# p7 of the first triple among the a products, two multiplications set aside, mixed loads and an earlier hold, in a matmul-tanh-multiply kernel

## The chip, the cores and the metric

The kernel runs on one core of a Trainium2 chip. The metric is the device time of one execution in microseconds (us); the time of a kernel is the median of its runs.

## The reference

```python
# x: (16, 512, 1024), w1, w2: (1024, 768), all float32
y1 = np.matmul(x, w1)
y2 = np.matmul(x, w2)
return (np.tanh(y1) * y2).astype(np.float32)
```

## The kernel before

**Tiles.** The 16 * 512 = 8192 rows of x are 64 row tiles of 128 rows. The 1024 terms of the inner dimension are 8 chunks of 128 (`k`), in two halves of four. The columns of the two weights make three blocks of 512: `a` (the first 512 columns of w1), `b` (the first 512 of w2) and `g` (the last 256 of w1 and of w2 side by side). Operands are fp16, sums are fp32 in eight PSUM banks.

**Two ways to multiply.** The first four row tiles (`HEAD`) are multiplied plainly, chunk by chunk, in chains `a`, `g`, `b` (`mm`, L421; the b chain of row tile 3 is kept for the very end). The other 60 make 20 triples. Three row tiles by two halves of the inner dimension by three column blocks would be 18 products of half an inner dimension each; a bilinear scheme does it in 15 (`p0` to `p14`, four matmuls each, `product`, L444). Its operands are sums of x blocks (`A_SUMS`, made by VectorE per triple, `x_sum`, L412) and sums of weight blocks (`B_SUMS`, made once, `w_sum`, L403). A number names a block or a sum: for x, bits 0 to 5 are the two halves of the triple's three row tiles; for weights, bits 0, 1, 2 are a, b, g of the first half and bits 3, 4, 5 of the second. So p7 (16 by 1) takes the first half of the triple's third row tile and block a; p10 (32 by 8) that tile's second half and block a; p6 (15 by 5) needs all of the first two row tiles, and no b; p1 (3 by 24) needs the second half of b.

**After the products.** A product goes to a bank (`c0` to `c10`). `C_OPS` lists what is made of it: copies from a bank to the SBUF buffer `arena` (`copy376` takes p7's result, ScalarE, L448), additions (`add312` adds that copy to p6's result, in front of p9; VectorE, L454), tanh (ScalarE, L457) and the multiplications `m0`, `m1`, `m2`, `mh0`... by the other half (VectorE, L462). Plain chains have their own: tanh L424, multiplication L428; for row tiles 0 to 2 the b result is copied to a buffer `y` (L431) and multiplied much later (`later_mul`, L435).

**Loads.** SP's queue loads the first four row tiles in halves as float32 (`x00` is row tile 0, first half) and the a and g weights into slots of `arena`; ScalarE's queue loads a0 to a3. VectorE and ScalarE cast them (L359, L357; `cx..`, `ca..`, `cg..`). POOL's queue loads the b weights and all other row tiles, cast to fp16 on the way (L350, L353), first the eight b, then row tiles 6, 4, 5 (`rows_in`), then 7, 8, 9 and on. In front of the first b load POOL waits for the cast of g0 (`gate`, L484), and from row tile 10 on it waits in front of each load (`hold_loads`, L481, a copy of one column) for the transposed tile four before, here T7.

**Transposes.** x must be turned. Row tiles 0 to 6 are turned by TensorE (L371) and copied from PSUM (`evacuate`, L357); from 7 on by DMA from SP's queue (`T7`, ..., L378), in order of row tiles.

**Order.** Nothing here is a loop in the program. A planner in Python (`Planner`) gets every operation with its engines, cost, due time, `needs` and `behind`, simulates the engines, and the instructions are written out in the order it finds. The order of the products on PE is given as a list (`plan.strict`): `FIRST_ORDER` for the first triple from `START`, `PE_ORDER` for the others, where "+" means one triple later. Plain matmuls and transposes are fitted in by the planner. `hold` is the earliest time of an operation in the plan, `lands` when a load is assumed to land. On the chip each engine runs its instructions in the written order and waits on semaphores.

Beside this ScalarE makes sums of absolute values of all inputs (`D..`, `aw..`, L381), which a flag at the end checks.

Of the kernel before, what the change touches and what calls it, by code (L numbers as in the profile page):

```python
# [69 lines left out]
FIRST_ORDER = "7 10 1 6 12 9 11 14 8"  # L70
# [156 lines left out]
def kernel(  # L227
# [14 lines left out]
    F = 512  # L242
# [10 lines left out]
    LANDING = {HEAD + 6: 5.8, HEAD + 7: 4.1, HEAD + 8: 3.9}  # L253
    S_AHEAD, HALVED = 4.0, 4
    LATER = {mt: 66.0 + 13.0 * mt for mt in range(HEAD - 1)}
# [25 lines left out]
    S_NAMES = [o[3] for o in C_OPS if o[1] in ("copy", "add") and o[3][0] == "s"]  # L281
    arena = once.tile([P, len(S_NAMES) * C_BUFS * F], f32, name="arena")
# [3 lines left out]
    early_x = once.tile([P, len(A_SUMS) * S_BUFS * KH * P // 2], f32, name="early_x")  # L286
    x_first = [early_x[:, mt * K:(mt + 1) * K] for mt in range(HEAD)]
# [8 lines left out]
    def xh_place(mt):  # L296
        return (mt - HEAD) % XH_BUFS

    def xh_before(mt):
        return next((m for m in range(mt - 1, 1, -1) if xh_place(m) == xh_place(mt)), None)  # L300
# [35 lines left out]

    def load_first(e, mt, h):
        pin(nc.sync.dma_start(x_first[mt][:, half(h)], xf[mt][:, half(h)]))

    def cast_x(e, mt, h):  # L340
        copy(e, xh(mt)[:, half(h)], x_first[mt][:, half(h)])
# [10 lines left out]
    def load_x(e, mt):  # L352
        pin(nc.gpsimd.dma_start(xh(mt), xf[mt]))  # L353
# [87 lines left out]

    def product(e, i, dst, a, b, begins):
        for k in range(KH):
            pin(nc.tensor.matmul(place(i, dst), x_operand(i, a)[:, k, :], w_rhs(b, k),  # L444
                                 start=begins and k == 0, stop=k == KH - 1, skip_group_check=True))
# [17 lines left out]

    def flag_1(e):
        pin(nc.vector.tensor_scalar(good, sums, HIGH, None, ALU.is_le))
# [14 lines left out]
    def hold_loads(e, mt):  # L480
        pin(nc.gpsimd.tensor_copy(held, xt(mt)[:, 0, :1]))  # L481

    def gate(e, s, k):
        pin(nc.gpsimd.tensor_copy(held, w_cols(s, k)[:, :1]))  # L484
# [5 lines left out]
    START = 28.6  # L490
    ORIGIN = START - 6 * SLOT

# [17 lines left out]
    GATE = ("g", 0)  # L510
    in_order = on_sp[4:] + late + [f"x{mt}" for mt in rows_in]
# [3 lines left out]
    for n in in_order:  # L515
        now += 1.25 if n in in_order[-3:] else size[n[0]]
        lands[n] = now + (LAG if now > LAG_FROM else 0.0)
# [3 lines left out]
    for n, what in enumerate(on_sp):  # L521
        before = [f"L{on_sp[n - 1]}"] if n else []
        if what[0] == "x":
            op(f"L{what}", {"sp": 0.05}, 0.1 * n - 100, [], load_first, int(what[1]), int(what[2]), issued=before, lands=lands[what])
        else:
            s, k = what[0], int(what[1])
            j = slices.index((s, k))
            old = [slices[i - SLOTS] for i in range(j, j + 1 + (s == "g")) if i >= SLOTS]
            op(f"L{what}", {"sp": 0.05}, 0.1 * n - 100, [], load_w, s, k, int(what[2]) if s == "g" else None, issued=before,
               behind=[f"c{a}{b}" for a, b in old], lands=lands[what])  # L530
    op("gate", {"pool": 0.1}, 0.0, ["c%s%d" % GATE], gate, *GATE)
    for n, what in enumerate(late):
        op(f"c{what}", {"pool": 0.58}, 0.1 * n, [], load_w, "b", int(what[1]), issued=[f"c{late[n - 1]}" if n else "gate"], lands=lands[what])
    for n, mt in enumerate(rows_in):
        op(f"L{mt}", {"pool": 0.58}, 1 + 0.1 * n, [], load_x, mt, issued=[f"L{rows_in[n - 1]}" if n else f"c{late[-1]}"],
           behind=[f"cx{m}{h}" for m in range(2, HEAD) for h in range(2) if xh_place(m) == xh_place(mt)], lands=lands[f"x{mt}"])
# [7 lines left out]
    all_casts = [f"c{s}{k}" for s, k in slices if s != "b"]  # L544
# [19 lines left out]
    for mt in rows_in:  # L564
        for h in range(2):
            by_pe(mt, h, lands[f"x{mt}"] - 2, f"L{mt}")
# [17 lines left out]
    def reuse_out(mt):  # L584
        return [f"st{mt - O_BUFS}"] if mt >= HEAD + O_BUFS else []
# [81 lines left out]
    for i in range(TRIPLES):  # L667
# [10 lines left out]
        for o in C_OPS:  # L678
# [10 lines left out]
            if kind in ("seed", "copy", "add"):  # L689
                before = []  # L690
                if o[3][0] == "s":
                    before = [f"{r}.{i - C_BUFS}" for r in readers[o[3]]] if i >= C_BUFS else all_casts
# [8 lines left out]
            if kind in ("t", "th"):  # L701
                lo, n = (0, F) if kind == "t" else (F, G)
                op(f"{name}.{i}", {"act": 0.5 if n == F else 0.285}, due, needs, c_tanh, i, r, o[4], lo, n, o[5],
                   behind=reuse_out(mt) + ([f"{FIRST_READER[name]}.{i}"] if i == TRIPLES - 1 and name in FIRST_READER else []), chains=chains)
            elif kind == "m" and i < HALVED:
# [7 lines left out]
    for mt in range(MT):  # L713
        i = (mt - HEAD) // 3 if mt >= HEAD else -1
        if mt < HEAD:
            kept = mt == HEAD - 1
            for t in range(2 if mt < 2 else 0):
                op(f"st{mt}{'ag'[t]}", {"sp": 0.05}, 1e3, outs[mt][t:t + 1], store, mt, t * F, (F, G)[t], behind=[f"p12.{11 + 2 * mt}"], xfer=0.5)
            if mt >= 2:
                op(f"st{mt}", {"sp": 0.05}, 1e3, outs[mt][:1] if kept else outs[mt], store, mt, F if kept else 0, G if kept else N, behind=[f"p12.{11 + 2 * mt}"], xfer=1.0)  # L720
# [10 lines left out]
    for mt in range(BY_PE, MT):  # L731
        back = xh_before(mt)
        free = [] if back is None else ([f"PT{back}0", f"PT{back}1"] if back < BY_PE else [f"T{back}"]) + ([f"D{back}"] if back >= HEAD else [])
        before = f"L{mt - 1}" if mt > BY_PE else f"L{rows_in[-1]}"
# [4 lines left out]
        op(f"T{mt}", {"sp": 0.05}, None, [f"L{mt}"], transpose, mt, issued=[f"T{mt - 1}"] if mt > BY_PE else [],  # L739
           behind=xt_readers[mt - XT_BUFS] if mt >= XT_BUFS and mt - XT_BUFS != HEAD - 1 else [], xfer=1.2, latency=LANDING.get(mt, 1.0 if mt < HEAD + 6 else 3.0))  # L740
    for mt in range(HEAD, MT):
        i, r = divmod(mt - HEAD, 3)
        soon = START + 6 + 1.1 * r if i == 0 else slot_of[i, "p7"] + (2, 0, -4, -8)[min(i, 4) - 1] + 4.3 * r
        op(f"D{mt}", {"act": 1.05}, soon + 4, [f"L{mt}"], abs_x, mt, hold=soon)
# [124 lines left out]
```

## Time and profile before

| | |
|---|---|
| median of 3 runs | 297.62 us (297.62 to 297.82) |
| profiled execution | 297.88 us |
| its span, first to last instruction | 296.3 us |
| PE busy | 289.6 us, 98% of the span |
| VectorE (DVE) busy | 257.4 us, 87% |
| ScalarE (ACT) busy | 226.3 us, 76% |
| GpSimd (POOL) busy | 49.2 us, 17% |
| granted TensorE clock, mean | 0.997 |
| DMA | 63.51 MB, mean 214 GB/s |

PE is TensorE, SP is SyncE, whose work is to issue DMAs. A row of the timeline gives start, duration, engine, line of the kernel, operation, output<-inputs, shapes and count; instructions of one kind that follow each other are one row. In brackets stands the idle time ahead of the row and what ended it. Matmuls are pipelined: a row's duration reaches to the modelled end of its last matmul and overlaps the next row, so the pace is read from the starts. A row of a group (`xcount | busy, mean | idle`) gives busy us, mean ns of one, and idle us before them. A row of the windows gives stretch, its length, and each engine's busy us with counts, for PE, PEld, DVE, ACT, POOL. An issue row ends with the us from issue to landing.

### The profile page before, as it was taken

What the parts mean: (1) busy time and instruction counts of PE and PEld (TensorE: products, weight loads), DVE (VectorE), ACT (ScalarE), POOL (GpSimd) and SP (SyncE); (2) the same over time, 40 slices, a digit from 0 to 9 for tenths busy, and PEclk for the clock granted to TensorE, in tenths of its full rate; (3) what the DMA queues carried; (4) which work ended last, traced back from release to release, by engine and by line L of the source; (5) the groups of instructions that cost most, each with busy time, mean ns of one, the idle gap of its engine ahead of it and who ended that gap; (6) DMA issues with size and microseconds to landing.
All of it is one profiled execution on the core that took longest, in us unless ns stands there. A gap on an engine that the chain in (4) does not pass through costs nothing. (4 is left out here: it accounts for less than half of the span.)

```text
span 296.3 us, 4677 instructions
## 1 busy us (share of the span) xinstructions
PE 289.6 (98%) x1374; PEld 131.9 (45%) x1374; DVE 257.4 (87%) x552; ACT 226.3 (76%) x453; POOL 49.2 (17%) x129
## 2 busy tenths in 40 slices
PE   7999999999999999999999999999999999999994
PEld 3344444444444444444444444444444444444442
DVE  1679899989999998888989898898989989898785
ACT  3586899699978979797797988768686776868442
POOL 0063033020213021102110120031012110000000
PEclk9999999999999999999999999999999999999998
DMA  6999999999999999999999999999999999340334
GB/s 215 388 307 204 183 160 149 229 197 237 224 253 271 215 198 252 237 144 253 233 234 162 221 191 218 195 310 223 221 235 232 261 269 298 127 162 25 136 141 164
DMA packets 84715, 63.51 MB, mean 214 GB/s; under 512 B 62800, under 2 KB 66896, under 8 KB 84688
## 3 DMA queue, kind: packets, MB, share of 16 engines
q1 hardware_dynamic: 73888, 44.84, 62.9%
q0 software_dynamic: 9792, 16.78, 37.2%
q10 hardware_dynamic: 1008, 1.57, 1.5%
q8 instruction: 11, 0.18, 0.3%
q14 instruction: 16, 0.13, 0.2%
HBM read 39.85 MB, written 25.17 MB: 219 GB/s over the span
## 5 line engine op out<-in xcount | busy, mean ns | idle before, releaser
L444 PE MATMUL bank<-b,early_x 128*128 128x512 f16 x640 | 148.3, 379 | 0.1
L444 PEld LDWEIGHTS <-early_x 128*128 128x128 f16 x800 | 78.1, 98 | 95.0 <-issue 0.7
L454 DVE TENSOR_TENSOR bank<-bank,arena 128x512 f32<-128x512 f32 x100 | 69.6, 697 | 14.4 <-ACT arena L448 8.8
L448 ACT ACTIVATE arena<-bank 128x512 f32<-128x512 f32 x100 | 59.4, 596 | 28.7 <-PE bank L444 28.5
L462 DVE TENSOR_TENSOR o<-o,bank 128x256 f32<-128x256 f32 (+1 forms) x132 | 64.3, 512 | 6.1 <-ACT o L457 5.4
L381 ACT ACTIVATE junk<-xh 128x1024 f16<-128x1024 f16 x60 | 63.3, 1054 | 0.2
L444 PEld LDWEIGHTS <-xT 128*128 128x128 f16 x400 | 39.0, 98 | 46.6 <-issue 0.3
L444 PE MATMUL bank<-b,xT 128*128 128x512 f16 x240 | 58.3, 379 | 0.0
L457 ACT ACTIVATE o<-bank 128x256 f32<-128x256 f32 (+1 forms) x80 | 34.5, 436 | 16.0 <-DVE bank L454 11.7
L444 PE MATMUL bank<-wh,xT 128*128 128x512 f16 x160 | 41.1, 379 | 0.0
L444 PE MATMUL bank<-wh,early_x 128*128 128x512 f16 x160 | 40.9, 379 | 0.0
L481 POOL CAST held<-xT 128x1 f32<-128x1 f16 x54 | 12.3, 227 | 159.4 <-DMA xT<-xh 159.3
L353 POOL DMA_DIRECT2D xh<-in_x_dram x60 | 31.9, 532 | 17.2 <-issue 7.7
L412 DVE TENSOR_TENSOR early_x<-early_x,xT 128x512 f16<-128x512 f16 x80 | 33.2, 419 | 0.5
L448 ACT ACTIVATE bank<-bank 128x512 f32<-128x512 f32 x40 | 21.5, 574 | 7.3 <-DVE bank L454 6.2
L457 ACT ACTIVATE o<-arena 128x512 f32<-128x512 f32 x40 | 25.1, 628 | 1.2 <-DVE arena L454 1.2
L421 PE MATMUL bank<-wh,xT 128*128 128x512 f16 x72 | 18.5, 379 | 0.5 <-DVE wh L359 0.3
L412 DVE TENSOR_TENSOR early_x<-xT,xT 128x512 f16<-128x512 f16 x40 | 16.8, 419 | 0.0
L412 DVE TENSOR_TENSOR early_x<-xT,early_x 128x512 f16<-128x512 f16 x40 | 16.8, 419 | 0.0
L454 DVE TENSOR_TENSOR bank<-arena,bank 128x512 f32<-128x512 f32 x20 | 13.9, 695 | 2.4 <-ACT o L457 0.9
L454 DVE TENSOR_TENSOR arena<-bank,arena 128x512 f32<-128x512 f32 x20 | 13.7, 683 | 0.2
L454 DVE TENSOR_TENSOR arena<-arena,bank 128x512 f32<-128x512 f32 x20 | 13.6, 681 | 0.0
(47 smaller groups left out, 134.7 us busy)
## 6 DMA issues: line engine op xcount, KB each, us to landing
out_dram<-o SPq DMA_DIRECT2D x58, 384.0 KB, 5.3
xh<-in_x_dram POOLq DMA_DIRECT2D x60, 256.0 KB, 6.8
arena<-in_w_dram SPq DMA_DIRECT2D x12, 256.0 KB, 5.6
early_x<-in_x_dram SPq DMA_DIRECT2D x8, 256.0 KB, 5.0
arena<-in_w_dram ACTq DMA_DIRECT2D x4, 256.0 KB, 5.9
wh<-in_w_dram POOLq DMA_DIRECT2D x8, 128.0 KB, 5.1
out_dram<-o SPq DMA_DIRECT2D x4, 256.0 KB, 6.5
xT<-xh SPq DMA_TRANSPOSE x57, 6.9
```

What stands on the lines that cost most here:

```text
L353: pin(nc.gpsimd.dma_start(xh(mt), xf[mt]))
L381: pin(nc.scalar.activation(junk[:, :src.shape[-1]], src, ACT.Abs, scale=scale, accum_out=sums[:, column:column + 1]))
L412: pin(engine[e].tensor_tensor(x_operand(i, v), x_operand(i, a), x_operand(i, b), OP[how]))
L421: pin(nc.tensor.matmul(bank(chain)[:, :rhs.shape[-1]], xt(mt)[:, k, :], rhs, start=first, stop=k == KO - 1, skip_group_check=True))
L444: pin(nc.tensor.matmul(place(i, dst), x_operand(i, a)[:, k, :], w_rhs(b, k), start=begins and k == 0, stop=k == KH - 1, skip_group_check=T ...
L448: pin(nc.scalar.activation(place(i, dst), place(i, src), ACT.Copy, scale=float(sign)))
L454: pin(nc.vector.tensor_tensor(place(i, dst), a, b, ALU.add if signs == (1, 1) else ALU.subtract))
L457: pin(nc.scalar.activation(out_tile(HEAD + 3 * i + r)[:, lo:lo + n], place(i, src)[:, :n], ACT.Tanh, scale=float(sign)))
L462: pin(nc.vector.tensor_tensor(o, o, place(i, src)[:, at:at + n], ALU.mult))
L481: pin(nc.gpsimd.tensor_copy(held, xt(mt)[:, 0, :1]))
```

## The change

- p7 of the first triple leaves `FIRST_ORDER`, is no longer in the strict list and gets the time 13.0 in the plan, among the plain a products. For it the first half of row tile 6 (`x60`) is loaded as float32 by SP, behind x01, into a slot of `arena` (`STAGED`), and cast by VectorE. `copy376`'s buffer changes its place in `arena`, and buffers wait only for the casts of the slots they lie on.
- The first triple's products follow as 10 6 1 12 ... instead of 7 10 1 6 12 ...
- POOL loads b0 b4 b1 b5 x61 x4 b2 x51 x50 b6 b3 b7 instead of all b and then 6, 4, 5. Row tile 5 comes in two halves.
- Row tiles of the second triple come in the order 7, 9, 8 (`TURNS`), in loads, transposes and buffers. The load of row tile 10 is held until the load of row tile 8 has landed, not until T7; later holds wait for the tile that is four before in the new order.
- `m0` and `m2` of the first triple: ScalarE copies the result from its bank into the output buffer of row tile 11 or 10, not in use yet, and VectorE multiplies from there, from 55 and 54 us of the plan on, as one instruction of 512 columns in place of two of 256 that read the bank.
- Some plan constants follow (`LANDING`, the `D` holds of the second triple), and row tile 0 is stored in one piece.

```diff
-FIRST_ORDER = "7 10 1 6 12 9 11 14 8"
+FIRST_ORDER = "10 6 1 12 9 11 14 8"
...
-    LANDING = {HEAD + 6: 5.8, HEAD + 7: 4.1, HEAD + 8: 3.9}
+    TURNS = (2, 0, 1), (0, 2, 1)
+    LANDING = {7: 35.9, 9: 37.4, 8: 38.8, 10: 47.3, 11: 48.1, 12: 49.0, 13: 51.2, 14: 58.2}
+    rows = list(range(HEAD)) + [HEAD + 3 * i + r for i in range(TRIPLES) for r in (TURNS[i] if i < len(TURNS) else (0, 1, 2))]
+    turn = {mt: n for n, mt in enumerate(rows)}
...
+    ASIDE = {"m0": (HEAD + 7, 55.0), "m2": (HEAD + 6, 54.0)}
...
+    S_NAMES.insert(1, S_NAMES.pop(0))
...
+    STAGED = SLOTS - 2
...
+    def x_staged(mt, h):
+        return x_first[mt][:, half(h)] if mt < HEAD else arena[:, STAGED * F:(STAGED + 1) * F]
...
+    def slot_casts(name):
+        n = S_NAMES.index(name) * C_BUFS
+        return [f"c{s}{k}" for j, (s, k) in enumerate(slices) if s != "b" and n <= j % SLOTS < n + C_BUFS] + [f"cx{HEAD + 2}0"] * (n <= STAGED < n + C_BUFS)
...
+    def c_aside(e, r, src, borrowed):
+        pin(nc.scalar.copy(out_tile(borrowed)[:, :F], place(0, src)))
+
+    def aside_mul(e, r, borrowed):
+        o = out_tile(HEAD + r)[:, :F]
+        pin(nc.vector.tensor_tensor(o, o, out_tile(borrowed)[:, :F], ALU.mult))
...
-    def hold_loads(e, mt):
-        pin(nc.gpsimd.tensor_copy(held, xt(mt)[:, 0, :1]))
+    def hold_loads(e, name):
+        mt = int(name[1:])
+        pin(nc.gpsimd.tensor_copy(held, xt(mt)[:, 0, :1] if name[0] == "T" else xh(mt)[:, :1]))
...
+    P7 = 13.0
...
+    position["p7", 0] = 0
...
-    plan.strict = [f"{p}.{i}" for _, i, p in sequence]
+    plan.strict = [f"{p}.{i}" for _, i, p in sequence if (p, i) != ("p7", 0)]
+    slot_of[0, "p7"] = P7
...
-    on_sp = "x00 x10 x20 x30 x01 x11 a4 a5 x21 a6 x31 a7".split() + [f"g{k}{t}" for k in range(KH) for t in range(2)]
-    late = [f"b{k}" for s, k in slices if s == "b"]
-    rows_in = (HEAD + 2, HEAD, HEAD + 1)
+    on_sp = "x00 x10 x20 x30 x01 x60 x11 a4 a5 x21 a6 x31 a7".split() + [f"g{k}{t}" for k in range(KH) for t in range(2)]
+    by_pool = "b0 b4 b1 b5 x61 x4 b2 x51 x50 b6 b3 b7".split()
+    GATES = {"b0": ("cg0", w_cols("g", 0)[:, :1])}
...
+            elif i == 0 and name in ASIDE:
+                borrowed, at = ASIDE[name]
+                op(f"y{name}.0", {"act": 0.5}, due + 1, [n for n in needs if n[0] != "t"], c_aside, r, o[4], borrowed, chains=chains)
+                op(f"{name}.0", {"dve": 0.6}, at + 6, [f"y{name}.0"] + [n for n in needs if n[0] == "t"], aside_mul, r, borrowed, hold=at)
...
-    for mt in range(BY_PE, MT):
-        back = xh_before(mt)
+    for n, mt in list(enumerate(rows))[BY_PE:]:
+        back, last, held_by = xh_before(mt), rows[n - 1], f"T{rows[max(n - AHEAD, BY_PE)]}"
...
-        if mt >= BY_PE + FREE:
-            op(f"H{mt}", {"pool": 0.1}, None, [f"T{max(mt - AHEAD, BY_PE)}"], hold_loads, max(mt - AHEAD, BY_PE), issued=[before])
+        if n >= BY_PE + FREE:
+            if n == BY_PE + FREE:
+                held_by = f"L{rows[BY_PE + FREE - 1]}"
+            op(f"H{mt}", {"pool": 0.1}, None, [held_by], hold_loads, held_by, issued=[before])
```

More of the change, by code (lines that the diff above doesn't have):

```diff
@@ L296, in xh_place @@
     def xh_place(mt):
-        return (mt - HEAD) % XH_BUFS
+        return (turn[mt] - HEAD) % XH_BUFS
     def xh_before(mt):
-        return next((m for m in range(mt - 1, 1, -1) if xh_place(m) == xh_place(mt)), None)
+        return next((m for m in rows[turn[mt] - 1:1:-1] if xh_place(m) == xh_place(mt)), None)
     pin = tc.keep_in_program_order
@@ L514 @@
     now = 9.2
-    for n in in_order:
-        now += 1.25 if n in in_order[-3:] else size[n[0]]
+    for n in arrivals:
+        now += 1.25 if n in by_pool and n[0] == "x" and len(n) == 2 else size[n[0]]
         lands[n] = now + (LAG if now > LAG_FROM else 0.0)
@@ L563 @@
         op(f"D{mt}", {"act": 1.05}, START + 8, [f"Lx{mt}0", f"Lx{mt}1"], abs_x, mt, hold=11 + 4 * mt)
[L564 removed]
+    for mt in rows[HEAD:BY_PE]:
         for h in range(2):
[L566 removed]
+            by_pe(mt, h, x_loads[mt, h][1] - 2 - 0.1 * h * (mt == HEAD + 1), x_loads[mt, h][0])
     def made(mt):
```

69 lines of the change are left out of this document (43 added, 26 removed).

## The prediction

> **What bounds the kernel now.** I read the page first, then the waits and the timeline of PE, then, where PE was late, the timelines of the engines that feed it.
>
> ```profile
> span 296.3 us, 4677 instructions
> PE 289.6 (98%) x1374; PEld 131.9 (45%) x1374; DVE 257.4 (87%) x552; ACT 226.3 (76%) x453; POOL 49.2 (17%) x129
> ```
>
> PE is busy for 98% of the span, and the change neither adds nor removes a matmul. So the time can change only by the stretches in which PE waits. The view of waits for PE names three, 1.9 us together, but it lists only waits in which PE was wholly idle. The starts of the rows show the rest:
>
> ```profile
> 12.37 1.03 PE L421 MATMUL bank<-wh,xT 128*128 128x512 f16 x4
> 13.52 0.40 PE L371 MATMUL bank<-ident_h,xh 128*128 128x128 f16 x4
> 14.19 1.02 PE L421 MATMUL bank<-wh,xT 128*128 128x512 f16 x4 [0.27 <-DVE wh L359]
> 15.05 0.39 PE L371 MATMUL bank<-ident_h,xh 128*128 128x128 f16 x4
> 15.27 1.11 PE L421 MATMUL bank<-wh,xT 128*128 128x512 f16 x4
> 16.22 1.03 PE L421 MATMUL bank<-wh,xT_kept 128*128 128x512 f16 x4
> 17.15 1.24 PE L421 MATMUL bank<-wh,xT 128*128 128x512 f16 x5
> ...
> 24.09 4.91 PE L421 MATMUL bank<-wh,xT 128*128 128x512 f16 x22
> 28.84 0.61 PE L371 MATMUL bank<-ident_h,xh 128*128 128x128 f16 x8
> 29.29 0.59 PE L421 MATMUL bank<-wh,xT 128*128 128x512 f16 x2
> ...
> 32.34 4.92 PE L444 MATMUL bank<-b,early_x 128*128 128x512 f16 x20
> ...
> 38.85 1.03 PE L444 MATMUL bank<-wh,xT 128*128 128x512 f16 x4
> 39.71 1.03 PE L444 MATMUL bank<-b,xT 128*128 128x512 f16 x4
> ...
> 43.17 4.48 PE L444 MATMUL bank<-b,early_x 128*128 128x512 f16 x20
> ```
>
> A product of four matmuls starts 0.86 us after the one before (38.85, 39.71), 0.216 us per matmul; eight transposes take 0.45 us (28.84 to 29.29). Between 12.37 and 17.15 stand 16 matmuls (3.45) and 8 transposes (0.45), 3.90 us of work in 4.78: **0.88 us of idle**. The two rows of 20 matmuls tell the second place: 4.92 us against an undisturbed 4.48, so **0.44 us** between 32.34 and about 37. From there on the rows follow each other without a gap. These 1.32 us are all that this change can reach, since what comes before 12 us precedes the moved work.
>
> The first idle belongs to the loads:
>
> ```profile
> 11.41 0.43 DVE L359 CAST wh<-arena 128x512 f16<-128x512 f32 x1 [0.25 <-DMA arena<-in_w_dram]
> 12.08 0.43 DVE L359 CAST wh<-arena 128x512 f16<-128x512 f32 x1 [0.24 <-DMA arena<-in_w_dram]
> ...
> 16.67 0.43 DVE L359 CAST wh<-arena 128x512 f16<-128x512 f32 x1 [1.15 <-DMA arena<-in_w_dram]
> ```
>
> Each cast starts when its 256 KB arrive, 0.67 us apart, and 17.15 on PE starts when the cast of 16.67 (g0) is done. So loads set PE's pace until 17.15.
>
> **p7 of the first triple, moved to 13 us.** Work moved before 17.15: 4 matmuls (0.86) and the 4 transposes of x60 (half of 0.45), 1.08 us. The price is x60 in SP's queue ahead of x11, a4 to a7 and all g: each arrives 0.67 later, g0's cast ends at 17.77 instead of 17.10. By work alone, PE would be at that point at 17.15 - 0.88 + 1.08 = 17.35; by the loads at 17.82, which is later and counts. PE is 0.67 late there with 1.08 of later work already done: **gain 0.41 us**. The cast of x60 (0.43 like its neighbours) fits between DVE's casts, which leave 0.25 idle each; ACT gives one eviction and copy376 earlier than before. copy376 may go then because its slots of the arena held a2 and a3 and no longer wait for every cast.
>
> **Loads mixed, p6 ahead of p1.** On POOL's queue three b loads (b6, b3, b7) now stand behind row tile 5, and half of row tile 6 has left it:
>
> ```profile
> 17.55 4.38 POOL L350 DMA_DIRECT2D wh<-in_w_dram  x8
> wh<-in_w_dram POOLq DMA_DIRECT2D x1, 128.0 KB, 4.0
> wh<-in_w_dram POOLq DMA_DIRECT2D x1, 128.0 KB, 5.5
> 24.03 1.06 POOL L353 DMA_DIRECT2D xh<-in_x_dram  x2 [1.05 <-DMA wh<-in_w_dram]
> xh<-in_x_dram POOLq DMA_DIRECT2D x1, 256.0 KB, 6.6
> 34.63 0.69 DVE L454 TENSOR_TENSOR bank<-bank,arena 128x512 f32<-128x512 f32 x1
> ```
>
> The first b load (issued at 17.55, 4.0 us) landed at 21.6; the last (issued about 21.34, the end of the eight, less one issue of 0.55; 5.5 us) at 26.8: 0.75 apiece. Row tile 5 (24.03, 6.6 us) landed at 30.6. It loses three b (2.2) and half a row tile (0.6) ahead of it, and gains the 0.67 of x60: some 2.1 us earlier, 28.5. Before, p6 could start 2.9 us after that landing (33.5: transposes, evictions, sums 11 and 15); the same lag gives 31.4. PE comes to it at 24.09 + 0.67, plus all 24 b matmuls (5.18), 20 of the 24 transposes (1.1) and p10 (0.86), about 31.9. So PE's wait for sum 15 goes. What is late next is b7, at about 30.7 (30.6 + 0.67 for x60 - 0.6 for the half that left; the queue ends there), before 31.9 as well, and weight sum 24 for p1, which p6 ahead of it covers. The second part of the 0.44 was p9, which followed p6 after one product and waited for add312 (34.63 + 0.69 = 35.32); with two products between there is 0.86 more room. **Gain 0.44 us**, bounded by 0 (another wait of the same size) and 0.44. POOL gets one issue more (0.53), and the gate stays.
>
> **The two multiplications set aside.**
>
> ```profile
> L462 DVE TENSOR_TENSOR o<-o,bank 128x256 f32<-128x256 f32 x84 | 33.4, 416 | 5.5 <-ACT o L457 5.1
> L435 DVE TENSOR_TENSOR o<-o,y 128x512 f32<-128x512 f32 x3 | 2.1, 685 | 0.0
> L431 ACT COPY y<-bank 128x512 f32<-128x512 f32 x3 | 1.6, 624 | 0.0
> 40.00:45.00 5.00, 5.00 (x25) 2.28 (x24) 5.00 (x13) 4.82 (x10) 0.53 (x1) 1.00 1.18 188
> 50.00:60.00 10.00, 10.00 (x48) 4.43 (x46) 9.95 (x26) 7.24 (x15) 1.58 (x6) 1.00 1.10 205
> ```
>
> DVE loses four half multiplications (33.4 / 84 = 0.40 each, 1.6 us) in a stretch where it is full (5.00 of 5), and gets two of 0.685 back after 54 us. ACT gets two copies of 0.62. On PE this is worth nothing by itself, since PE does not wait there; it is what lets DVE follow a PE that comes earlier. DVE needs it: its weight sums begin behind g0's cast, 0.67 later. What hides ACT's copies is that its sums of absolute values can move. Without such room, for these or for p7's eviction, one copy of 0.62 stands in front of PE and takes the first gain.
>
> **The hold of row tile 10, and the order 7, 9, 8.**
>
> ```profile
> 25.41 1.18 POOL L353 DMA_DIRECT2D xh<-in_x_dram  x2 [0.32 <-issue]
> 36.38 0.37 POOL L481 CAST held<-xT 128x1 f32<-128x1 f16 x1 [9.79 <-DMA xT<-xh]
> xh<-in_x_dram POOLq DMA_DIRECT2D x1, 256.0 KB, 8.3
> xh<-in_x_dram POOLq DMA_DIRECT2D x1, 256.0 KB, 4.1
> 31.89 17.37 SPq L378 DMA_TRANSPOSE xT<-xh  x7
> L378 SPq DMA_TRANSPOSE xT<-xh x1: 1260/1260/1260, 33.4 to 33.4; - x1
> DMA to landing us min/median/max: 3.7/3.7/3.7
> L378 SPq DMA_TRANSPOSE xT<-xh x1: 1344/1344/1344, 41.0 to 41.0; - x1
> DMA to landing us min/median/max: 7.1/7.1/7.1
> 37.89 0.69 DVE L403 TENSOR_TENSOR b<-b,b 128x1024 f16<-128x1024 f16 x1
> ```
>
> POOL waited 9.79 us for T7; behind that hold stood the loads of 10 and all later tiles. Now it waits for the last initial load (the second of the issues at 25.41, so 26.06, and 8.3 us: 34.4), so load 10 issues at 34.9 instead of 36.9, and at 4.1 us lands near 39. T9 takes T8's place as second transpose: issued at 33.4, 3.7 us, 37.1. Its reader p7.1 (38.85) moves to 38.0. Lead 0.9; nothing lost.
>
> **Sum.** 0.41 + 0.44 = 0.85 us, both behind 12 us and ahead of work that has no gaps to absorb it. The profiled execution took 297.88 us (span 296.3 and 1.6 around it), 0.26 above the median of 297.62: 297.03 for the one, **296.8 us** for the median. I call 0.2% (0.6 us) what a measurement of this kernel can tell from no change.
>
> **Rivals.** *DVE cannot follow (chance 0.22).* Weight sum 27, which p0 of the first triple needs, ends at 37.89 + 0.69 = 38.58, 1.1 ahead of 39.71. With DVE 0.67 late it ends at 39.25, and PE wants it at 38.86: 0.4 of the 0.85 is lost again, 297.2; if more such sums stand that near, up to no gain, 297.6. Against it: DVE sat idle 0.63 us at 36.28, waiting for T7, and could use that time for these sums.
>
> *Load 10 slows the transposes (0.16; this one ends slower).* T10, issued at 41.0 while the loads that POOL's holds release from 36.9 on were under way, took 7.1 us, against 3.7 for the second transpose. If load 10 does that to T9, it lands at 33.4 + 7.1 = 40.5, and p7.1 stalls 2.5 us: 297.62 - 0.85 + 2.5 = 299.3. It makes the kernel slower from a landing later than 38.85. Against it: load 10's bytes move in the last 2 of its 4.1 us, from about 37, when T9 is nearly through.
>
> *Queues take turns (0.1).* If load and transpose share evenly, T9 is held up by no more than load 10's own time, 1.25 us (row tile 5 landed at 30.6 and 9 at 34.4, three loads later), lands at 38.35, and costs 0.35: 297.1. This is the rule of the Trainium skill, "DMA: Bandwidth & Descriptors", section Queues, rings and completion order: each DMA engine goes round the queue rows that have work, a packet at a time. The trace does not decide it: the 3.7 and the 7.1 us differ in the loads beside them, but no row counts their turns.
>
> *The move does nothing (0.04).* If the planner's order lets p7 run only after the loads have caught up, x60's 0.67 is paid and nothing filled: 297.62 + 0.67 - 0.44 = 297.9.
>
> **How the numbers follow.** The forecast has 0.48. Its own range is 296.3 (all of the 1.32) to 297.0. Range: 296.3 to 297.7, which takes in all but the slower rival and tails of the others. Faster by over 0.2% (below 297.02): the forecast and most of the turns rival with the low end of DVE's, 0.61; same 0.21; slower 0.18.
>
> **What would show it.** In the profile after: four L444 matmuls on PE before 16 us; the first g row on PE near 17.8; the row of products after p10 without excess over 0.216 us per matmul; row tile 5's transposes before 30 us; POOL's first hold ending near 34.5; p7.1 (wh, xT) near 38.0 and the spacing unbroken from there. I am wrong if PE's rows between 36 and 62 us show gaps: released by xT if the transposes are late, by DVE if the sums are. If g's first row is at 17.8 but p10 is later than 27.5, the b stage took the gain.

## The result, and the profile after

The kernel takes **300.34 us** after the change (median of 10 runs, 297.49 to 311.56) against 297.82 us before (10 runs on the same chip, 297.62 to 304.66). Without the disturbed executions, the ratio after to before is 1.0047, 95% interval 1.0029 to 1.0064: slower by about half a per cent. The forecast was 296.8 us and faster, so it was wrong, and the result lies outside the range. Before, most executions lie within 0.3 us; after, they spread over some 5 us. The profiled execution of after is its fastest, 297.49 us, and hides most of the loss.

The page of after, span and the first part (busy us, share of the span, instructions):

```profile
span 295.9 us, 4682 instructions
PE 289.3 (98%) x1374; PEld 132.6 (45%) x1374; DVE 255.8 (86%) x552; ACT 224.2 (76%) x454; POOL 52.4 (18%) x130
```

PE's work is the same. Its timeline after, at the places that the forecast named:

```profile
12.99 1.03 PE L457 MATMUL bank<-wh,xT 128*128 128x512 f16 x4
...
17.74 1.03 PE L430 MATMUL bank<-wh,xT 128*128 128x512 f16 x4
...
28.55 0.39 PE L380 MATMUL bank<-ident_h,xh 128*128 128x128 f16 x4
28.79 1.02 PE L457 MATMUL bank<-wh,xT 128*128 128x512 f16 x4
29.65 0.39 PE L380 MATMUL bank<-ident_h,xh 128*128 128x128 f16 x4
...
31.38 2.75 PE L457 MATMUL bank<-b,early_x 128*128 128x512 f16 x12
33.97 0.59 PE L430 MATMUL bank<-wh,xT 128*128 128x512 f16 x2
34.41 1.89 PE L457 MATMUL bank<-b,early_x 128*128 128x512 f16 x8
36.16 1.02 PE L457 MATMUL bank<-wh,early_x 128*128 128x512 f16 x4
...
37.89 1.03 PE L457 MATMUL bank<-wh,xT 128*128 128x512 f16 x4
38.75 1.03 PE L457 MATMUL bank<-b,xT 128*128 128x512 f16 x4
39.61 1.03 PE L457 MATMUL bank<-wh,early_x 128*128 128x512 f16 x4
41.02 1.04 PE L457 MATMUL bank<-b,early_x 128*128 128x512 f16 x4 [0.38 <-DVE early_x L421]
```

p7 of the first triple runs at 12.99, the first g row at 17.74, row tile 5 is transposed at 28.55 and 29.65, and from 31.38 to 36.16 the starts lie 0.216 us per matmul apart (12 matmuls in 2.59, 8 in 1.75). p7 of the second triple starts at 37.89 instead of 38.85: **0.96 us gained**, where 0.85 was forecast. PE has done the same work in both kernels at that point, 124 fp16 matmuls of 512 columns and 48 fp16 transposes. Then comes what the forecast did not have: p6 of the second triple should start at 40.48 (39.61 + 0.86) and starts at 41.02. It lacks a sum of blocks of row tiles 7 and 8; a gap between 36 and 62 us released by VectorE (DVE) was the sign that the forecast named for being wrong. VectorE's timeline:

```profile
39.87 0.42 DVE L421 TENSOR_TENSOR early_x<-early_x,xT 128x512 f16<-128x512 f16 x1 [0.94 <-DMA xT<-xh]
```

VectorE had been waiting for a transpose, T8, now the third. POOL's timeline:

```profile
34.80 0.88 POOL L502 CAST held<-xh 128x1 f32<-128x1 f16 x1 [6.08 <-DMA xh<-in_x_dram]
35.62 0.53 POOL L362 DMA_DIRECT2D xh<-in_x_dram  x1
```

POOL's hold ends near 35.6 and lets the load of row tile 10 go, beside T8. The DMA issues of after between 35.5 and 36.1 us (size, us from issue to landing) put the two side by side:

```profile
xh<-in_x_dram POOLq DMA_DIRECT2D x1, 256.0 KB, 4.9
xT<-xh SPq DMA_TRANSPOSE x1, 4.8
```

T8, issued at 35.06, took 4.8 us. The load, issued 1.3 us earlier than before (36.89), landed at 40.55, only 0.4 earlier.

### The profile page after: what moved, and what is told of

Same layout as the page of the kernel before. It is cut to its first block, busy times and chain, and to the rows that moved or that the text cites. A ratio compares the mean times of both kernels' runs of the same rounds, so it can differ in the third digit from the quotient of the medians.

```text
span 295.9 us, 4682 instructions
## 1 busy us (share of the span) xinstructions
PE 289.3 (98%) x1374; PEld 132.6 (45%) x1374; DVE 255.8 (86%) x552; ACT 224.2 (76%) x454; POOL 52.4 (18%) x130
## 5 line engine op out<-in xcount | busy, mean ns | idle before, releaser
L461 ACT ACTIVATE arena<-bank 128x512 f32<-128x512 f32 x100 | 57.7, 595 | 16.3 <-PE bank L457 16.2
L475 DVE TENSOR_TENSOR o<-o,bank 128x256 f32<-128x256 f32 (+1 forms) x128 | 61.7, 513 | 6.4 <-ACT o L470 4.2
L457 PE MATMUL bank<-wh,xT 128*128 128x512 f16 x160 | 41.0, 379 | 0.0
L502 POOL CAST held<-xT 128x1 f32<-128x1 f16 x53 | 14.4, 272 | 100.2 <-DMA xT<-xh 100.2
L430 PE MATMUL bank<-wh,xT 128*128 128x512 f16 x72 | 19.4, 380 | 0.3 <-ACT xT L366 0.2
L390 ACT ACTIVATE junk<-wh 128x768 f16<-128x768 f16 x16 | 13.6, 848 | 0.0
```

Of the source, the lines that this page charges most:

```text
L390: pin(nc.scalar.activation(junk[:, :src.shape[-1]], src, ACT.Abs, scale=scale, accum_out=sums[:, column:column + 1]))
L430: pin(nc.tensor.matmul(bank(chain)[:, :rhs.shape[-1]], xt(mt)[:, k, :], rhs, start=first, stop=k == KO - 1, skip_group_check=True))
L461: pin(nc.scalar.activation(place(i, dst), place(i, src), ACT.Copy, scale=float(sign)))
L475: pin(nc.vector.tensor_tensor(o, o, place(i, src)[:, at:at + n], ALU.mult))
L502: pin(nc.gpsimd.tensor_copy(held, xt(mt)[:, 0, :1] if name[0] == "T" else xh(mt)[:, :1]))
```

## The experiments

In the expectations "tail" is the time from the start of the last matmul to the end of the span: the stores of the last results lie there. PE ends with eight matmuls of 0.11 us in one row, so it is the span less that row's start and 0.77.

**The change once more, longer.**

> The changed kernel once more, to see whether its spread belongs to it and where a longer execution loses its time. All theories expect the spread again (297.5 to above 300 us, against 0.3 us for the kernel before). Theory H (the earlier hold): row tile 10's load runs beside the transposes of 7, 9 and 8; in a longer execution T8 or T9 lands later than the 39.84 and 37.03 us of the profiled one, and PE's gap in front of p6 of the second triple (0.54 us there) is longer by as much as the time. Theory L (a head without slack): the gaps are before 36 us, at products that wait for loads or their evictions. Theory S (steady part): the gaps are after 60 us.

Measured: 300.46 us (12 runs, 299.16 to 312.93), ratio 1.0071 (1.0040 to 1.0102). The profiled execution took 299.55 us, nearer to the median than the first. Its rows on PE:

```profile
41.60 1.04 PE L457 MATMUL bank<-b,early_x 128*128 128x512 f16 x4 [0.90 <-DVE early_x L421]
...
291.30 1.04 PE L430 MATMUL bank<-wh,xT_kept 128*128 128x256 f16 x8
```

Its DMA view from 292.2 to 294.5 us, with the instruction queue `q8` (packets, MB, share of 16 engines) and the issues:

```profile
q8 instruction: 1, 0.02, 2.4%
out_dram<-o SPq DMA_DIRECT2D x2, 128.0 KB, 3.7
out_dram<-o ACTq DMA_DIRECT2D x1, 128.0 KB, 3.7
```

T8, beside the load, took 5.3 us here. The gap ahead of p6 is 1.06 us (41.60; 40.54 was due), which takes back the whole gain: PE's last matmul starts at 292.06 against 291.90 before. The rest of the loss lies *behind* PE. The span ends 5.83 us after that start (4.36 before), because the last three stores take 3.7 us each, where such stores took 2.1 to 2.2 in the profiles of before and after. Beside them runs one 16 KB packet of `q8`, at 294.2. (In the profile of after that packet ran at 289.5, and three earlier stores beside it took 3.3 us, where those in their place took 2.1 before.) So of this execution's 1.67 us over the profile of before, 0.16 is on PE and 1.47 in the tail.

**The hold alone put back to T7.**

```diff
+        name = "T7" if name[0] == "L" else name
```

> The changed kernel with one operand altered: the hold in front of row tile 10's load reads a column of T7 again, as before the change, in place of row tile 8's load. The order of all instructions stays. Theory H: T8 lands near 38.3 instead of 39.84, no gap in front of p6 of the second triple, 296.8 us and a spread of some 0.3 us. Theories L and S: the spread stays, the median near 300.

Measured: 298.68 us (297.58 to 312.33), ratio 1.0025 (0.9988 to 1.0061); profiled 298.63. PE's timeline:

```profile
37.98 1.03 PE L457 MATMUL bank<-wh,xT 128*128 128x512 f16 x4
38.84 1.03 PE L457 MATMUL bank<-b,xT 128*128 128x512 f16 x4
39.70 1.03 PE L457 MATMUL bank<-wh,early_x 128*128 128x512 f16 x4
40.57 1.03 PE L457 MATMUL bank<-b,early_x 128*128 128x512 f16 x4
...
290.36 1.04 PE L430 MATMUL bank<-wh,xT_kept 128*128 128x256 f16 x8
```

T8 in the view of the transposes' line (issues, and us to landing):

```profile
L387 SPq DMA_TRANSPOSE xT<-xh x1: 1257/1257/1257, 35.0 to 35.0; - x1
DMA to landing us min/median/max: 3.2/3.2/3.2
```

The DMA view from 291.5 to 293.5 us:

```profile
q8 instruction: 1, 0.02, 2.7%
out_dram<-o SPq DMA_DIRECT2D x2, 128.0 KB, 3.7
out_dram<-o ACTq DMA_DIRECT2D x1, 128.0 KB, 3.7
```

The load of row tile 10 goes at 36.32, T8 takes 3.2 us, and the gap is gone. PE is 0.87 us ahead of before at p7 and still 0.78 ahead at its last matmul (291.12 instead of 291.90). So the first steps' gain lasts; but this execution, too, has a `q8` packet beside the last stores, and its tail is 5.85. By the times alone the two kernels do not part, since their intervals overlap; what shows the hold is the gap, and the next run.

A load let go only 0.7 us earlier does this because it begins to move just before T8 is through and not just after. In the traces the load's first packet starts at 37.77 with the hold on T7, behind T8's last one (37.68). In the change it starts at 37.50, and T8's remaining packets come between those of the load, the last at 39.47.

**The early hold alone, in the kernel before** (on the load of row tile 9, there the third).

```diff
-        pin(nc.gpsimd.tensor_copy(held, xt(mt)[:, 0, :1]))
+        holds.append(mt)
+        pin(nc.gpsimd.tensor_copy(held, xh(9)[:, :1] if len(holds) == 1 else xt(mt)[:, 0, :1]))
```

> The kernel before with one operand altered the other way: the first hold, in front of row tile 10's load, reads a column of row tile 9's load, the last of the initial ones, in place of T7. Theory H: T9, the third transpose, lands 1 to 2 us later than its 38.1, p7 of the second triple (38.85) waits for it, and the time rises by 0.5 to 2 us and spreads. Theories L and S: 297.6 us, spread 0.3.

Measured: 302.0 us (299.18 to 308.51), ratio 1.0109 (1.0075 to 1.0144); profiled 299.18. PE's timeline:

```profile
40.12 1.04 PE L444 MATMUL bank<-wh,xT 128*128 128x512 f16 x4 [1.16 <-DMA xT<-xh]
```

The hold needs nothing else of the change to lose time: the load goes at 34.84, the third transpose lands at 40.07 instead of 38.12. This profiled execution is the shortest of the twelve; of its 1.30 us over the profile of before, 1.28 are on PE. Where the longer ones lose the rest was not profiled.

**The change with the order 7, 8, 9**, so that the third transpose is p7's.

```diff
-    TURNS = (2, 0, 1), (0, 2, 1)
+    TURNS = (2, 0, 1), (0, 1, 2)
```

> The changed kernel with the second triple's row tiles in the order 7, 8, 9 in loads and transposes, all else planned anew. The hold then waits for row tile 9's load. Theory H: still spread, since the early load stays; now T9 is third, lands near 39.8 and stalls p7 of the second triple (37.9) by about 2 us: 299 us or more in every run. A theory by which the new order alone does the harm: 296.8 us and steady.

Measured: 302.47 us (300.94 to 304.75), ratio 1.0138 (1.0075 to 1.0202); profiled 303.41.

```profile
40.63 1.21 PE L457 MATMUL bank<-wh,xT 128*128 128x512 f16 x4 [2.35 <-DMA xT<-xh]
```

Whichever row tile stands third is late. The order 7, 9, 8 makes it the one that is needed last; it softens the hold's price from 2.5 us at p7 to the 0.5 to 1.1 at p6. The longer stall also costs more than its length: from 41.5 to 45 us the granted clock is 0.53, and eight matmuls from 41.63 on take 3.28 us instead of 1.73. (After the stall of 1.3 us in the run before this one the clock stayed at 1.00.) Another 2.1 us of this execution are in its tail (6.49), where a `q8` packet runs at 296.7.

**Is the tail a matter of the fetches?** `q8` has 11 packets of 16 KB in each of these executions, 22 to 32 us apart. If they are PE's instructions, 42 more PE instructions ahead of all else move each fetch against the work. The warm-up matmuls were cut into 28 of 128 columns in place of 7 of 512, in the kernel with the hold on T7, in the change, and in the kernel before as the control:

```diff
-    WARM = 512, 512, 512, 512, 512, 512, 512
+    WARM = (128,) * 28
```

> The changed kernel with the hold on T7, and PE's program 42 instructions longer at its start: the seven warm-up matmuls of 512 columns of constants are 28 of 128, the same columns, before the first data arrive. In the run with the hold on T7 PE was 0.78 us ahead of the kernel before at its end (last matmul at 291.12 against 291.90), and the time was not shorter because the last three stores landed 3.7 us after their issue in place of 2.1; a 16 KB packet of the queue of instructions started at 293.3 between them, where the kernel before has it at 288.6. Theory F (the instruction fetch hits the last stores): the shift puts the fetch some 4 us earlier against the work, the last stores land 2.1 us after issue, 296.9 us and steady. Theory D (the stores are late for a reason of the DMA queues themselves, or the spread comes from the transposes): still 298 to 299 us.

> The changed kernel with its own hold on row tile 8's load, with the same 42 instructions more at PE's start. Theory F with theory H: the fetch misses the last stores, the gap in front of p6 of the second triple (0.5 to 1.1 us) stays: 297.4 to 298.2 us. Theory D: 299 to 300 us as without the shift.

> Control: the kernel before with the same 42 instructions more at PE's start. Its fetch already lies ahead of the last stores. All theories: 297.6 us, within 0.3; if it moves, the shift itself costs or gains that much and is taken off the other two.

Measured: 301.11 us (299.01 to 306.15), ratio 1.0089 (1.0051 to 1.0127); 302.99 us (298.21 to 311.97), 1.0084 (1.0037 to 1.0130); and 299.52 us (298.69 to 303.86), 1.0046 (1.0025 to 1.0067). The last fetch moved to 290.1, 292.0 and 286.7, ahead of the last stores, and the tails are 4.38, 4.36 and 4.46, as expected. The times are not: the control itself is 0.46% slower. The *first* fetch now falls among the last g loads (17.9 to 18.8 instead of 21); in the control's profiled execution (298.69) the last two of these land 1.1 us later than before, and PE waits 0.8 us for the casts. In the first of the three:

```profile
22.18 1.76 PE L430 MATMUL bank<-wh,xT 128*128 128x512 f16 x6 [0.94 <-ACT wh L366]
```

This shift is therefore no clean test of the times. The first kernel, profiled at 302.15 us, has gaps at 244, 258 and 263 us as well, 2.9 us together, all released by ScalarE, which the profile of before does not have. The second, profiled at 304.14, has one of 3.7 us at 82, where ScalarE had waited for VectorE.

**The setting aside taken out**, on the first of these.

```diff
-    ASIDE = {"m0": (HEAD + 7, 55.0), "m2": (HEAD + 6, 54.0)}
+    ASIDE = {}
```

> As the first of these four (hold on T7, shifted start), but the two multiplications are not set aside: m0 and m2 of the first triple read their banks as before the change, all planned anew. The prediction's step, that setting them aside lets VectorE follow a PE that comes earlier: gaps of PE between 38 and 60 us, 0.3 to 0.8 us slower than with them aside. The rival, that VectorE had room anyway (0.6 us idle before): the same time within 0.2 us.

Measured: 300.04 us (299.75 to 303.34), ratio 1.0084 (1.0050 to 1.0118); profiled 300.23. VectorE does the four halves in front of PE again, with a gap of 1.19 us at 53.48 where the kernel with the setting aside has 0.54. On PE that step does what it was said to do. But the late gaps are gone as well, and by their times the kernels with and without it do not differ (ratios 1.0089 and 1.0084).

**A shift that leaves the start alone.** In the triple with i = 10 the 24 matmuls of six products are issued in two halves of 256 columns:

```diff
+    quota = {10: 6}
...
+        if quota.get(i, 0):
+            quota[i] -= 1
+            parts = [slice(0, F // 2), slice(F // 2, F)]
+            for part in parts:
+                pin(nc.tensor.matmul(place(i, dst)[:, part], x_operand(i, a)[:, k, :], w_rhs(b, k)[:, part],
```

In the four kernels that follow directly, the second half's start flag drops the first half's first term of a new sum; the work on PE is the same. Hold on T7, the change, and the kernel before with 120 and with 24 matmuls in halves:

> The changed kernel with the first hold on T7 and, in the triple with i = 10 (some 160 us in), the 24 matmuls of six products issued as two halves of 256 columns each: the same work, 24 instructions (48 records) more on PE, so that the instruction fetches from there on come some 5 us earlier against PE's work. Theory F (the 0.8 to 0.9 us that PE gains with the hold on T7 was lost only because the last fetch, a 16 KB packet at 293.3 us, fell among the last stores): the last fetch lies at 283 to 290, the last stores take 2.0 to 2.2 us each, tail after PE's last matmul 4.3 to 4.5; with 0 to 0.3 for the halves the profile is 297.0 to 297.4, and the timed ratio 0.997 to 0.999, with less spread than without the halves. Rival R (the loss is in what follows the store order of the change, not in the fetch): tail 5.8, time 298.5 to 298.9.

> The changed kernel itself (hold on the load of row 8) with the same 24 halves. Theory H and F together: the gap ahead of p6.1 stays (0.4 to 1.1 us, released by the sum of row 8), the tail is 4.3 to 4.5: 297.5 to 298.2, ratio 1.000 to 1.002, so 0.5 to 0.9 above the kernel with the hold on T7 and the same halves. Rival (the hold's loss was given back before the end, and only the fetch is slow): equal to that kernel within 0.2.

> The kernel before with 120 matmuls of the triples i = 9 and 10 issued as two halves each: 240 records more on PE, a little under one fetch distance (some 252), so that a twelfth fetch comes some 10 to 40 records ahead of PE's end, where the change has its eleventh. Theory F: this fetch lies at 290 to 295 and, where it falls among the last stores, they take 3.3 to 3.7 us and the tail is 5.3 to 5.9: 299.0 to 299.8 by the profile, ratio 1.003 to 1.006. If the fetch starts ahead of 290 the tail stays 4.4 and the time is 297.9 to 298.3. Rival R (the tail belongs to the changed order of stores): tail 4.4 wherever the fetch lies.

> The kernel before with the same 24 halves as the other two: the control for them. Its last fetch, at 288.6 us without them, moves to 280 to 287, where no wait depends on a transfer: tail 4.4, 297.7 to 298.2, ratio 1.000 to 1.001. If it is faster or slower by over 0.3 us, the halves or the later fetches have a price of their own, and it is taken off the other two.

| kernel | median us (range) | ratio (95%) | last `q8` fetch | tail |
|---|---|---|---|---|
| T7, 24 halves | 300.59 (297.38 to 301.59) | 1.0074 (1.0038 to 1.0111) | 288.4 | 4.37 |
| change, 24 halves | 298.83 (298.27 to 303.17) | 1.0036 (1.0022 to 1.0049) | 291.0 | 4.44 |
| before, 120 halves | 299.77 (298.01 to 305.45) | 1.0052 (1.0035 to 1.0069) | 300.2 | 5.95 |
| before, 24 halves | 297.88 (297.70 to 303.88) | 1.0005 (0.9996 to 1.0014) | 285.5 | 4.45 |

The control stands still. (The second and third kernel were profiled in their longest executions, 303.17 and 305.45 us.) In these four the tail follows the fetch and not the change: moved off, the tail is 4.4; and in the kernel before, where a twelfth packet lands among the last stores, they take 3.8 us and the tail is 5.95. But the first kernel's time was not as expected: the change, with its early hold, should have been slower than it by 0.5 to 0.9 us and is not. Two of its eight executions are at 297.38 and 297.73, six at 300.5 to 301.6, and the profiled one (300.48) has the late gaps again, 3.6 us in all. ScalarE's timeline there:

```profile
237.69 0.60 ACT L468 ACTIVATE arena<-bank 128x512 f32<-128x512 f32 x1 [0.49 <-PE bank L464]
240.71 1.15 ACT L477 ACTIVATE o<-arena 128x512 f32<-128x512 f32 x2 [2.42 <-DMA out_dram<-o]
```

ScalarE has a tanh to write, and its output tile is still being stored. The copy behind it (L468, 241.76) comes late, and PE waits for its bank. In most of the gaps of this kind ScalarE had waited for a store. They are not the change's alone: the change with 24 halves has some 5 us of them between 176 and 247 us, and the kernel before with 120 halves one of 3.3 us at 142, after ScalarE had waited 4.3 us for a store.

**Where do the late gaps come from?** One row further ahead for the loads from row 19 on (`AHEAD` 5 instead of 4), the setting aside out, and for the kernel before one row less and one more:

```diff
-        back, last, held_by = xh_before(mt), rows[n - 1], f"T{rows[max(n - AHEAD, BY_PE)]}"
+        back, last, held_by = xh_before(mt), rows[n - 1], f"T{rows[max(n - (5 if n >= 19 else AHEAD), BY_PE)]}"
```

> The changed kernel with the first hold on T7, 24 matmuls of the triple i = 10 in halves, and from row 19 on each load held for the transpose five rows back instead of four. Theory L (the late gaps come where the transposes run too short a way ahead of the products, so that stores queued behind them on SP land late and ACT waits for the output tile): the lead over the products from i = 10 on rises from 8 to 12 us to 14 or more, no gap over 0.2 us after 60 us, 296.9 to 297.4 by the profile, and the timed ratio 0.997 to 0.999. Rival S (the gaps are the chip's, in any kernel): most executions stay at 300 to 301. Rival X (more loads in flight delay the transposes of triples 5 to 8): gaps at 75 to 130 us, 298 to 300.

> The same kernel with loads held four rows back, as in the change, but the two multiplications not set aside (m0 and m2 of the first triple in halves from their banks, rows 4 and 6 stored earlier). If the setting aside shortens the lead (its stores stand together at 59.5 to 60.6 us, ahead of the transposes of rows 16 to 18): lead at i = 4 of 3.5 us or more instead of 1 to 2, lead from i = 10 on 13 us or more, no late gaps; against that a gap of 0.5 to 1.2 us at 46 to 54 us, where VectorE has the four halves to do: 297.4 to 298.3 by the profile. If it doesn't: lead as with it (8 to 12), late gaps in most executions, 300 to 301.5.

> The kernel before with each load from row 19 on held for the transpose three rows back instead of four. Theory L: the lead falls by about a row (4 us), from 13 to 16 us to 8 to 12 from i = 8 on, and with it gaps on PE released by ACT appear late, 0.5 to 4 us in all: 298.5 to 302, ratio 1.002 to 1.012. Rival S: the lead falls and nothing else changes, 297.6 to 298.0, ratio within 0.001 of 1.

> The kernel before with each load from row 19 on held five rows back, the control for the first of these: it has no late gaps to lose. Theory L: lead up by some 3 us, time 297.5 to 297.9, ratio within 0.001 of 1. If it is faster by 0.3 us or more, that much of the first run's gain is not from the change's own lead.

| kernel | median us (range) | ratio (95%) |
|---|---|---|
| T7, halves, 5 rows | 313.45 (306.09 to 318.87) | 1.0499 (1.0454 to 1.0545) |
| T7, halves, nothing aside | 298.53 (298.11 to 301.80) | 1.0028 (1.0002 to 1.0055) |
| before, 3 rows | 297.74 (297.61 to 305.64) | 0.9998 (0.9990 to 1.0007) |
| before, 5 rows | 304.15 (297.65 to 316.63) | 1.0016 (0.9993 to 1.0040) |

My theory L fell: loads further ahead should have removed the gaps and made this kernel far slower instead, and a row less costs the kernel before nothing. The first kernel's shortest execution, the profiled one (306.09), waits 3.3 us for transposes at 79 and 106 us, as rival X had it, and 5.2 us for ScalarE after 200 us. (The control with five rows has no measurable difference by its ratio; six of its twelve executions are at 308 to 317, and why was not followed up. The kernel before with three rows, profiled at 305.64, has a gap of 5.8 us at 170, after ScalarE had waited 6.8 us for a store.) By this, what counts is less how far the transposes run ahead of the products than what is in flight together; that is an inference from the landing times. The stores of 100 to 270 us (count, KB, median us to landing) in the kernel before:

```profile
out_dram<-o SPq DMA_DIRECT2D x42, 384.0 KB, 5.3
```

In the kernel with the hold on T7 and 24 halves, loads four rows ahead:

```profile
out_dram<-o SPq DMA_DIRECT2D x43, 384.0 KB, 6.7
```

With five rows it is 7.3 us, with nothing aside 5.6: of these kernels, the two in which the stores land latest have the late gaps. (The order is not strict: in the profile with the hold on T7 alone the stores take 6.4 us, and it has no late gap.) Without the setting aside none is left, and eight of twelve executions lie between 298.11 and 298.68; in exchange VectorE holds PE up, by 0.88 us:

```profile
52.07 1.02 PE L464 MATMUL bank<-wh,xT 128*128 128x512 f16 x4 [0.72 <-DVE o L482]
```

Why setting aside two multiplications should crowd the stores shows on SP's queue, before and after:

```profile
49.37 0.51 SPq L418 DMA_DIRECT2D out_dram<-o  x1
...
58.78 0.53 SPq L418 DMA_DIRECT2D out_dram<-o  x1
59.41 2.94 SPq L378 DMA_TRANSPOSE xT<-xh  x2
62.45 1.05 SPq L418 DMA_DIRECT2D out_dram<-o  x2
```

```profile
60.02 1.59 SPq L427 DMA_DIRECT2D out_dram<-o  x3
61.71 2.72 SPq L387 DMA_TRANSPOSE xT<-xh  x1
64.49 0.57 SPq L427 DMA_DIRECT2D out_dram<-o  x1
```

Row tiles 4 and 6 can be stored only after their multiplications at 54 and 55 us. The store that went at 49.4 now goes with two others at 60, ahead of a transpose. With nothing aside it goes at 49.78 again. But the three stores also stand together, at 59.51, in the profile with the hold on T7 alone, which has no late gap, and no run shows how a crowd at 60 us would last until 240. That the late gaps go with the setting aside is shown in two pairs of profiles; the way from one to the other is argued.

**The loads held closer**, three rows from row 31 of the load order on: in the kernel with the hold on T7 and 24 halves, and in the change.

> The changed kernel with the first hold on T7, 24 matmuls of the triple i = 10 in halves, and from row 31 of the load order on each load held for the transpose three rows back instead of four. Theory C (loads in flight crowd the stores, whose late landing stops ACT and then PE): the median store lands in 6.0 us or less instead of 6.8, no wait of ACT for a store over 1 us, no gap on PE over 0.2 us after 60 us, most executions 296.9 to 297.5, ratio 0.997 to 0.999: faster than both kernels. Rival B (the bunched stores of rows 4 and 6 keep the queue late whatever the loads do): most executions 299 to 301 as with four rows. Rival X (the transposes get too late for their products): gaps on PE released by the transposes at 130 to 200 us, 298 to 300.

> The change itself with the same closer hold from row 31 on. Theory C: what stays is the gap at p6.1 (0.5 to 1.1 us) and in many executions the last fetch among the last stores (1.5 us), while the executions over 299.6 go: 297.4 to 299.5, median 298.2 to 299.2, ratio 1.001 to 1.005. Rival B: as the change, median 300 to 300.5, spread 297.5 to 312.

Measured: 297.61 us (296.90 to 300.70), ratio 1.0004 (0.9976 to 1.0031), six of twelve executions between 296.90 and 297.45, where none of 23 of before was under 297.66; and 299.56 us (297.92 to 302.42), 1.0047 (1.0009 to 1.0086). In the first the stores of 100 to 270 us land in 5.6 us, the last ones in 2.1 to 2.2. Its profiled execution (298.88) has one gap over 0.2 us after 30 us, of 0.9 us:

```profile
78.58 1.02 PE L464 MATMUL bank<-wh,xT 128*128 128x512 f16 x4 [0.75 <-ACT o L477]
```

Theory C holds for the late gaps in this execution: nothing after 79 us is lost. The gap at 78.58 may be rival B's: in front of it VectorE waited 2.03 us for a transpose, and the transposes of that time stand behind the three stores of 60 us. So this version is no clear gain, but in its better half it reaches the 296.8 us that the forecast had for the change. On the change itself the median came out above what was expected, and six of twelve executions are still over 299.6, which theory C expected to go. Its profiled execution has no late gap, but T8 took 5.9 us, p6 waited 1.84, and the tail was 5.03.

## Why the prediction was wrong

**Right: p7 and the mixed loads.** The steps of 0.41 and 0.44 stand, with 0.96 us instead of 0.85 at p7 of the second triple (0.49 of it at the first g row), and 0.78 left at PE's end once the hold is put back. The time of the first g row was partly luck: the forecast had it wait for g0, whose cast was to end at 17.77. That load landed only 0.32 us later than before instead of 0.67 (16.90 after 16.58), its cast ended at 17.42, and PE came to the row at 17.74 by its own work.

**Wrong: the hold, "lead 0.9; nothing lost".** T9 landed at 37.03 (37.1 forecast) and p7 ran at 37.89 (38.0). But the step stopped there, and this is where the forecast failed. T8 had moved to third place and its reader, p6, was not looked at. Before, T8 landed as second transpose at 37.1; now at 39.8 to 41.0, and its sum and p6 with it: 0.54, 1.06 and 1.84 us in the three profiles of this kernel and of that with the loads held closer late. The rival *load 10 slows the transposes* had the mechanism and put it on T9, which was already through; it should have had more than 0.16. Its argument against itself, that the load's bytes move only when T9 is nearly through, held for T9 and not for T8, which was still under way. The rival of turns bounded the delay by the load's own time, 1.25 us. The runs show 1.6, 2.1 and 2.7 us for T8 (4.8, 5.3 and 5.9 against 3.2 with the hold on T7), so the bound doesn't hold here. The rule of the Trainium skill that the rival leaned on ("DMA: Bandwidth & Descriptors", section Queues, rings and completion order) has the DMA engines take turns between queues, a packet at a time. The traces agree in that T8's packets come between the load's; the bound was the rival's own. It counted one load, but the next one was issued only 1.1 us behind (36.76). Which part of the delay is the second load's, no run separates.

**Left out: the stores behind the setting aside, "worth nothing by itself".** On the engines it is worth 0.65 to 0.9 us, as the gaps at 52 to 54 us show when it is taken out: that cover was argued rightly. The working left out the stores that wait for the moved multiplications and then stand in front of the transposes near 60 us. In the kernel with the halves late gaps take 3.6 us of the profiled execution, and they go with the setting aside; that the crowded stores are the link is not shown. For the change itself no cost is shown: neither of its profiles has late gaps, and where its executions at 300 to 303 us lose their time stays open.

**Missing: the tail.** The forecast said that the time can change only by the stretches in which PE waits, so no term of the sum lay behind PE's end. Where a fetch falls among the last stores it is a lottery of about 1.5 us (0.7 to 2.1 in the profiles that have it), which an edit draws anew by shifting instructions, and which differs between executions of one kernel: two of the change had it at 289.5 and at 294.2.

**Not what decided:** *DVE cannot follow* shows only where the setting aside is taken out; *the move does nothing* is refuted by the rows at 12.99 and 17.74.

## What to carry to other kernels

When a queue is reordered or a load let go earlier, follow every transfer in it to its first reader, above all the one that moved back, and not only the one whose reader is next. A multiplication moved later takes its store along: look at what the store will stand in front of. And with PE at 98%, a gain of 0.3% is no larger than what a changed order of transfers or an instruction fetch in the tail can take, so judge it from many executions and not from one profile.

## What the runs showed of the hardware

- The packets of `q8` are PE's instructions: 48 or 240 more records on PE shift them, and 240 bring a twelfth. The Trainium skill, "Runtime: NRT & Kernel Launch", section Instruction fetch mechanics, has 16 KB blocks of 256 instructions, which agrees with some 252 records from packet to packet here, on average. It calls the cost mostly hidden. On PE it is: no gap stands at a fetch by itself. For transfers in flight it isn't: 128 KB stores go from 2.1 to 2.2 us to 3.7, and to 4.4 in one execution. But a late tail needs no such packet: two profiles without one there have tails of 4.85 and 5.04. What lengthened those is open; an 8 KB packet of the other instruction queue lies there, as it does in tails of 4.4.
- A DMA transpose took 4.8 to 5.9 us instead of 3.2 when a 256 KB load began to move before it was through, with a second load behind it.
- Loads let go one row further ahead took the kernel with the 24 halves from 1.0074 to 1.0499 times the kernel before (medians 300.6 and 313.5 us), with the same order of products; in the profiles the stores then landed in 7.3 us instead of 6.7, and the transposes in 9.7 instead of 7.9. On the kernel before, the same step shows no difference by its ratio (1.0016).
- After PE had stood still for about 2.5 us the granted clock was 0.53 for 3.5 us (the change with the order 7, 8, 9); after 1.3 us, and after 2.1 us in the kernel with five rows, it stayed at 1.00.
